# S5 input tables: the two subtractions per table half moved from VectorE into accumulating transposes on TensorE

## The chip, the cores and the metric

The kernel runs on one core of one Trainium2 chip. The metric is the device time of one execution in microseconds (us). TensorE is PE in the profile, its weight loads are PEld; VectorE is DVE, ScalarE is ACT, GpSimd is POOL, and SyncE, whose queue issues all the DMAs here, is SP or SPq.

## The reference, cut to what matters

One layer of a diffusion backbone on 256 latent and 256 context tokens of width 2048: an S5 mixer (128 groups of 16 channels, 64 complex states each, two directions), a gated output product, and a squared-ReLU MLP.

```python
def s5_scan(u, lam_bar, b_bar, s0, reverse):
    bu = jnp.einsum('btgh,gph->btgp', u, b_bar)
    ...
    _, states = lax.associative_scan(_lin_rec_combine, (a, bu), axis=1, reverse=reverse)
...
    lam_bar, b_bar = s5_discretise(a_re[direction], a_im[direction], log_dt[direction], b_re[direction], b_im[direction])
    st_ctx = s5_scan(uc_ctx, lam_bar, b_bar, s0, reverse)
    s_ctx_final = st_ctx[:, 0] if reverse else st_ctx[:, -1]
    st_lat = s5_scan(uc_lat, lam_bar, b_bar, s_ctx_final, reverse)
    y_lat = y_lat + jnp.einsum('btgp,ghp->btgh', st_lat, c_mat).real
...
    z = jax.nn.gelu(y)
    a, g = jnp.split(z @ w_glu, 2, axis=-1)
    return a * jax.nn.sigmoid(g)
...
x_lat = x_lat + gt1 * rmsnorm(y_lat, norm_mix_post)
x_lat = x_lat + gt2 * rmsnorm(sq_relu_mlp(modulate(rmsnorm(x_lat, ...), sh2, sc2), w1, w2), norm_mlp_post)
```

## The kernel before, in words

The S5 mixer is computed in chunks of 8 tokens (L = 8), so a sequence is 32 chunks. For every chunk position the input matrix of a group is a power of the decay times the input weights; a table of these is built once for each group. The 128 groups are 16 blocks of 8, and a block is worked as two halves of 4 groups. Three units of 4, 6 and 6 blocks share one scan each. In the order in which data flows:

- **Powers.** `Qr` and `Qi` hold the real and imaginary powers (128 partitions x 16 blocks x 8 x 8); ScalarE copies them in place, blocks 0 and 1 first.
- **Input tables (`e`).** For a block, GpSimd makes `s1` = Qr + Qi (tile s1e) and the sum and difference `s2` of the input weights `bcb` (tile s2e). For a half, VectorE makes the complex product with three multiplications and two subtractions, five instructions of 128x512: `k1` = s1 * Br, e1 = Qr * s2[0], e0 = Qi * s2[1], then e0 = k1 - e0 and e1 = k1 - e1 (`e_op`, recorded at the helper's line 122; k1 appears as k).
- **Transposes and strips.** TensorE transposes the four 128x128 pieces of e0 and of e1 into a PSUM tile `tr` each (`e_tr`, line 623), which ScalarE copies to `et`. TensorE also multiplies the same pieces by the output weights `cbd` into `st` (`strip`, line 636); this goes through `sk`, a transpose `wps` (line 649) and `W` to DRAM (`wd`), and comes back as the table `it` of a pair of blocks in 8 DMAs (line 689).
- **Scan.** TensorE applies `et` to the tokens (`v`, line 706), ScalarE copies the results into `ctx` and `lat`, and VectorE runs the unit's scan: steps of three dependent instructions (`t`, add, add; lines 727 to 734), five levels over the context and then 31 single steps over the latent chunks.
- **Output.** VectorE makes the output tables `dx` (`dy` for the last two blocks; three multiplications per half, from `bcc`), ScalarE and GpSimd make the sums `sp`, and TensorE adds `it` and `dx` products in `y` (lines 798 and 800). A GELU and a transpose follow.
- **Weights.** Beside all this, weight tiles of 1 MB pass through three `raw` buffers: 64 items for the adaLN products (`ada`, lines 476 and 484) and the items of the gated product (`gb`: line 991 for the first 10 of them, 998 for the rest). The next load of a buffer waits until TensorE has used it. After the gated product comes the MLP.

The order of all instructions up to the MLP is set by a planner (`Plan`): each task has an engine, a duration in us, dependences, a priority, and rings, which stand for buffers that it takes and gives back. The planner runs a list schedule with these numbers and emits the tasks in its order; on the chip each engine then runs its own instructions strictly in that order. The task numbers are estimates in the program and not read from a trace. The ring `e` has 2 buffers, `k1` has 1, `dx` has 4.

Of the kernel before, what the change touches and what calls it, by code (L numbers as in the profile page):

```python
# [8 lines left out]
F32 = mybir.dt.float32  # L9
# [107 lines left out]
def _body(ctx, tc, nc, I, O):  # L117
# [111 lines left out]
    with psx:  # L229
# [55 lines left out]
        sk = ew.tile([128, L, 4, H], F32, name="sk")  # L285
        cbd = [ew.tile([128, 8, 2, 32], F32, name=f"cbd{n}") for n in range(2)]
# [101 lines left out]
        for dst, src in ((Qr, qr), (Qi, qi)):  # L388
            for lower in (True, False):
                q_copy(dst, src, lower, 0, 2)  # L390
        sr = sq.tile([128, C], F32, name="sr")
# [11 lines left out]
        for name, cap in (("ada", 1), ("ev", 1), ("bcb", 2), ("bcs", 2), ("bcc", 2), ("s1e", 2), ("s2e", 1), ("sd", 2), ("cbd", 2),  # L403
                          ("k1", 1), ("dd", 1), ("e", 2), ("et", 2), ("tr", 2), ("st", 1), ("v", 1), ("x", 2), ("yv", 1), ("sk", 1), ("W", 1), ("it", 1),
                          ("ctx", 1), ("lat", 2), ("dx", 4), ("sp", 2), ("z", 1), ("t", 1), ("it2", 1)):
            plan.ring(name, [0.0] * cap)
# [43 lines left out]
        pt = [add("ACT", 0.95, lambda d=d, s=s, g=g, l=l: p_copy(d, s, g, l), prio=PR["p"]) for d, s, g in ((Pr, pr, 1.0), (Pn, pi, -1.0)) for l in (True, False)]  # L450
        t = []
# [138 lines left out]
        def e_sums(b):  # L590
            Bv = bct.pop(("b", b))
            s1 = ew.tile([128, L, 8], F32, tag="s1e", bufs=2, name="s1e")
            tt(SE, s1, Qr[:, b], Qi[:, b], ALU.add)
# [3 lines left out]
            est[b] = Bv, s1, s2  # L597
# [6 lines left out]
        def e_op(b, hf, k):  # L604

            Bv, s1, s2 = est[b]
            hs = slice(hf * 4, hf * 4 + 4)
            n = [128, 4, L, H]
            if k == 0:
                est[b, hf] = (ew.tile([128, 4, L, H], F32, tag="k1e", bufs=1, name="k1"),  # L610
                              ew.tile([128, 2, 4, L, H], F32, tag="e", bufs=2, name="e"))
            k1, e = est[b, hf]
            if k < 3:
                o, p, c = ((k1, s1, Bv[:, 0]), (e[:, 1], Qr[:, b], s2[:, 0]), (e[:, 0], Qi[:, b], s2[:, 1]))[k]
                tt(V, o, p[:, :, hs].rearrange("p t g -> p g t").unsqueeze(3).to_broadcast(n), c[:, hs].unsqueeze(2).to_broadcast(n), ALU.mult)
            else:
                tt(V, e[:, k - 3], k1, e[:, k - 3], ALU.subtract)

        def e_tr(b, hf, r):
            e = est[b, hf][1]  # L620
            est["ps"] = pst("tr", 2)
            for gi in range(4):
                PE.transpose(est["ps"][:, gi * 128:(gi + 1) * 128], e[:, r, gi].rearrange("p s h -> p (s h)"), ident)  # L623
# [7 lines left out]
        def strip(b, hf):  # L631
            e = est[b, hf][1]
# [848 lines left out]
```

## Time and profile before

| | us |
|---|---|
| median of 3 runs (range) | 1312.68 (1308.35 to 1317.29) |
| the profiled execution's own time | 1313.43 |
| its span in the profile | 1311.7 |
| PE busy in the span | 1178.7 (90%) |
| DVE busy | 897.1 (68%) |
| ACT busy | 539.4 (41%) |
| POOL busy | 192.5 (15%) |

Busy shares are averages over very different stages. The input tables are made between 31.7 and 286.5 us of the span; the S5 mixer's last output product ends at 417.3 us, the gated product at 560 us, and the rest is the MLP. The change touches the first of these.

### The profile page before, as it was taken

What the parts mean: (1) busy time and instruction counts of PE and PEld (TensorE: products, weight loads), DVE (VectorE), ACT (ScalarE), POOL (GpSimd) and SP (SyncE); (2) the same over time, 40 slices, a digit from 0 to 9 for tenths busy, and PEclk for the clock granted to TensorE, in tenths of its full rate; (3) what the DMA queues carried; (4) which work ended last, traced back from release to release, by engine and by line L of the source; (5) the groups of instructions that cost most, each with busy time, mean ns of one, the idle gap of its engine ahead of it and who ended that gap; (6) DMA issues with size and microseconds to landing.
All of it is one profiled execution on the core that took longest, in us unless ns stands there. A gap on an engine that the chain in (4) does not pass through costs nothing.

```text
span 1311.7 us, 22524 instructions
## 1 busy us (share of the span) xinstructions
PE 1178.7 (90%) x9457; PEld 957.2 (73%) x9457; DVE 897.1 (68%) x1200; ACT 539.4 (41%) x731; POOL 192.5 (15%) x200
## 2 busy tenths in 40 slices
PE   4576884696898999989999999999999999999997
PEld 1454553452434688989999999999978888888885
DVE  8999999878878677765555565555655555655555
ACT  5442544242115534574333334333434444444443
POOL 4766344611322000030000000000000000000000
PEclk8588997798899999999999999999999999999998
DMA  7488868989986888816656666566656555555552
GB/s 269 148 213 295 316 245 195 307 307 196 260 227 168 319 346 324 317 66 224 234 219 245 217 220 250 209 242 223 230 189 224 192 193 184 182 185 188 192 192 97
DMA packets 74093, 296.68 MB, mean 226 GB/s; under 512 B 7164, under 2 KB 30588, under 8 KB 48520
## 3 DMA queue, kind: packets, MB, share of 16 engines
q1 hardware_dynamic: 73992, 295.25, 66.3%
q8 instruction: 74, 1.21, 0.4%
q14 instruction: 27, 0.22, 0.1%
HBM read 291.15 MB, written 4.07 MB: 225 GB/s over the span
## 4 chain that ended last, share of the span: by engine, by line
PE 74%; DMA 9%; DVE 5%; SPq 1%; ACT 1%; issue 1%; POOL 0%; DVEq 0%; POOLq 0%; ACTq 0%
PE m L1325 27%; PE o L1358 27%; PE gb L998 9%; DMA raw<-wk 4%; PE gb L991 3%; DMA it<-wd 2%; DMA raw<-wa 2%; DVE e L122 2%; SPq L689 1%; PE ada L484 1%; PE y L800 1%; PE v L706 1%; DMA bcc<-bc 1%; PE m L1247 1%; PE ada L476 1%
## 5 line engine op out<-in xcount | busy, mean ns | idle before, releaser
L122 DVE TENSOR_TENSOR wlo<-raw,whi 128x2048 fp32r<-128x2048 f32 x126 | 288.7, 2291 | 134.7 <-ACT whi L125 134.7
L1325 PE MATMUL m<-h,whi 128*128 128x256 f32 x1984 | 248.2, 283 | 0.0
L125 ACT ACTIVATE whi<-raw 128x2048 fp32r<-128x2048 f32 (+1 forms) x130 | 243.8, 1876 | 1.5 <-PE m L1247 1.5
L1325 PEld LDWEIGHTS m<-h,whi 128*128 128x128 f32 x1984 | 242.5, 192 | 0.0
L1358 PE MATMUL o<-wlo,hh 128*128 128x512 f32 x512 | 160.5, 395 | 0.2 <-DVE wlo L122 0.2
L1358 PE MATMUL o<-whi,hh 128*128 128x512 f32 x512 | 160.6, 395 | 0.0
L1358 PE MATMUL o<-whi,hl 128*128 128x512 f32 x512 | 160.5, 395 | 0.0
L1325 PE MATMUL m<-h,wlo 128*128 128x256 f32 x992 | 129.1, 283 | 0.0
L1325 PEld LDWEIGHTS m<-h,wlo 128*128 128x128 f32 x992 | 123.5, 192 | 0.0
L125 ACT ACTIVATE hh<-hid 128x512 fp32r<-128x512 f32 x64 | 40.5, 633 | 194.5 <-PE o L1358 194.5
L125 ACT ACTIVATE r<-m 128x256 f32<-128x256 f32 x64 | 24.6, 384 | 222.9 <-PE m L1325 221.1
L1358 PEld LDWEIGHTS o<-wlo,hh 128*128 128x128 f32 x512 | 95.9, 187 | 24.1 <-DVE wlo L122 0.6
L1358 PEld LDWEIGHTS o<-whi,hh 128*128 128x128 f32 x512 | 95.8, 187 | 24.2 <-ACT hh L125 0.8
L1358 PEld LDWEIGHTS o<-whi,hl 128*128 128x128 f32 x512 | 96.0, 187 | 23.5
L1297 DVE TENSOR_TENSOR hl<-hid,hh 128x512 fp32r<-128x512 f32 x64 | 44.3, 693 | 88.8 <-ACT hh L125 88.7
L1269 DVE TENSOR_TENSOR hid<-r,m 128x256 f32<-128x256 f32 x64 | 26.9, 421 | 91.9 <-ACT r L125 91.9
L991 PE MATMUL gb<-raw,xz 128*128 128x512 f32 x160 | 76.0, 623 | 2.4 <-DMA raw<-wg 2.3
L623 PE MATMUL tr<-ident,e 128*128 128x128 f32 x256 | 44.7, 315 | 30.9 <-DVE e L122 24.6
L998 PE MATMUL gb<-hi,zs 128*128 128x512 f32 (+1 forms) x288 | 70.1, 357 | 0.0
L484 PE MATMUL ada<-raw,cst 128*32 128x512 f32 x256 | 36.9, 654 | 35.4 <-DMA raw<-wk 35.4
L623 PEld LDWEIGHTS tr<-ident,e 128*128 128x128 f32 x256 | 32.5, 160 | 45.8 <-DVE e L122 21.4
L991 PEld LDWEIGHTS gb<-raw,xz 128*128 128x128 f32 x160 | 30.2, 197 | 46.5 <-issue 40.2
(202 smaller groups left out, 1613.2 us busy)
## 6 DMA issues: line engine op xcount, KB each, us to landing
raw<-w SPq DMA_DIRECT2D x128, 1024.0 KB, 4.8
raw<-wk SPq DMA_DIRECT2D x48, 1024.0 KB, 8.4
raw<-wa SPq DMA_DIRECT2D x32, 1024.0 KB, 7.4
raw<-wg SPq DMA_DIRECT2D x32, 1024.0 KB, 5.2
k<-wk SPq DMA_DIRECT2D x16, 1024.0 KB, 7.3
it<-wd SPq DMA_DIRECT2D x64, 128.0 KB, 6.9
xz<-xs SPq DMA_DIRECT2D x4, 1024.0 KB, 9.1
bcb<-bc SPq DMA_DIRECT2D x16, 128.0 KB, 8.9
```

The costliest lines, as they stand in the source:

```text
L122: eng.tensor_tensor(out=out, in0=a, in1=b, op=op)
L125: A.activation(out=out, in_=in_, func=f, **kw)
L476: PE.matmul(adab["a"][32 * j:32 * j + 32, :n], cst[:, 2 * kt:2 * kt + 32], w[:, e, j], start=(kt == 0), stop=(kt == KT - 1))
L484: PE.matmul(adab["k"][32 * j:32 * j + 32, :], cst[:, 2 * kt:2 * kt + 32], w[:, j * 512:(j + 1) * 512], start=(kt == k0), stop=(kt == KT - ...
L623: PE.transpose(est["ps"][:, gi * 128:(gi + 1) * 128], e[:, r, gi].rearrange("p s h -> p (s h)"), ident)
L689: S.dma_start(it[16 * s:16 * s + 16], wdt[b2][:, :, (7 - s) * H:(7 - s) * H + 128])
L991: PE.matmul(banks[p][nk * t + k], xz[kt // BQ][:, GQ * C + (kt % BQ) * T + t * 128:][:, :128], wt[:, (nk * e + k) * 512:(nk * e + k + 1) * ...
L998: PE.matmul(banks[p][nk * t + k][:, :wd], a, w[:, (nk * e + k) * wd:(nk * e + k + 1) * wd], start=ff, stop=ll)
L1269: V.tensor_tensor(out=hid[:, nt], in0=r, in1=ps, op=ALU.mult)
L1297: V.tensor_tensor(out=hl, in0=hid[:, 2 * i:2 * i + 2], in1=hh.bitcast(F32), op=ALU.subtract)
L1325: PE.matmul(ps, w[a][:, kt], (h2h, h2l)[b][:, kt], start=a == b == kt == 0, stop=a == 1 and kt == KT - 1)
L1358: PE.matmul(banks[nh][2 * t + k], w[2 + x][:, e, zz], w[y][:, e * 1024 + k * 512:e * 1024 + k * 512 + 512], start=f and n == 0 and e == es ...
```

## The change

VectorE no longer subtracts. The sums are formed where the pieces are transposed: for each 128x128 piece TensorE transposes k1 and then e on top of it into the same PSUM region, as an accumulating pair. So that a sum serves for the difference, the sum of powers is made with a minus sign, `Qs` = -Qr - Qi, for all blocks in two VectorE instructions (`q_sum`: blocks 0 and 1 at the start, ahead of the reduction `sr`, and blocks 2 to 15 as a task) in place of 16 additions on GpSimd. k1 and both e are then minus what they are to give, and the ScalarE copies out of `v` and `st` scale by -1. The strips take k1 and e as four terms in place of two. The rings change: `k1` has 2 buffers and is given back with `e` after the strips, `s1e` is gone, `dx` has 3 buffers in place of 4. The planner's numbers for the changed tasks change with them (0.43 to 0.9 for a transposing task, 0.57 to 0.8 for a strip), so the order changes throughout the S5 stage.

```diff
--- before.py
+++ after.py
@@ -283,6 +283,7 @@
         V.memset(cst, 0.0)
         V.memset(epst, EPS)
         sk = ew.tile([128, L, 4, H], F32, name="sk")
+        Qs = ew.tile([128, NB, L, 8], F32, name="Qs")
         cbd = [ew.tile([128, 8, 2, 32], F32, name=f"cbd{n}") for n in range(2)]
         for t in cbd:
             GP.memset(t, 0.0)
@@ -388,6 +389,13 @@
         for dst, src in ((Qr, qr), (Qi, qi)):
             for lower in (True, False):
                 q_copy(dst, src, lower, 0, 2)
+
+        def q_sum(b0, b1):
+
+            a, b, o = (w[:, b0:b1].rearrange("p b t g -> p (b t g)") for w in (Qr, Qi, Qs))
+            V.scalar_tensor_tensor(out=o, in0=a, scalar=-1.0, in1=b, op0=ALU.mult, op1=ALU.subtract)
+
+        q_sum(0, 2)
         sr = sq.tile([128, C], F32, name="sr")
         V.tensor_reduce(out=sr, in_=ssum.rearrange("p (a b) -> p b a", b=C), axis=mybir.AxisListType.X, op=ALU.add)
         sr2 = [pst("tr", 2, "sr2") for i in range(2)]
@@ -400,9 +408,9 @@
 
         plan = Plan({"DVE": 25.0, "ACT": 24.4, "Pool": 22.9, "PE": 25.8, "SP": 27.8, "X": 0.0})
         add = plan.add
-        for name, cap in (("ada", 1), ("ev", 1), ("bcb", 2), ("bcs", 2), ("bcc", 2), ("s1e", 2), ("s2e", 1), ("sd", 2), ("cbd", 2),
-                          ("k1", 1), ("dd", 1), ("e", 2), ("et", 2), ("tr", 2), ("st", 1), ("v", 1), ("x", 2), ("yv", 1), ("sk", 1), ("W", 1), ("it", 1),
-                          ("ctx", 1), ("lat", 2), ("dx", 4), ("sp", 2), ("z", 1), ("t", 1), ("it2", 1)):
+        for name, cap in (("ada", 1), ("ev", 1), ("bcb", 2), ("bcs", 2), ("bcc", 2), ("s2e", 1), ("sd", 2), ("cbd", 2),
+                          ("k1", 2), ("dd", 1), ("e", 2), ("et", 2), ("tr", 2), ("st", 1), ("v", 1), ("x", 2), ("yv", 1), ("sk", 1), ("W", 1), ("it", 1),
+                          ("ctx", 1), ("lat", 2), ("dx", 3), ("sp", 2), ("z", 1), ("t", 1), ("it2", 1)):
             plan.ring(name, [0.0] * cap)
         plan.ring("raw", [])
         for n in "bsc":
@@ -448,6 +456,7 @@
         lp_ = wk = drp = None
         qt = [add("ACT", 0.85, lambda d=d, s=s, l=l: q_copy(d, s, l, 2, NB), prio=1) for d, s in ((Qr, qr), (Qi, qi)) for l in (True, False)]
         pt = [add("ACT", 0.95, lambda d=d, s=s, g=g, l=l: p_copy(d, s, g, l), prio=PR["p"]) for d, s, g in ((Pr, pr, 1.0), (Pn, pi, -1.0)) for l in (True, False)]
+        qs = add("DVE", 1.05, lambda: q_sum(2, NB), qt, prio=0)
         t = []
         for m in range(5):
             for k in range(2):
@@ -589,12 +598,10 @@
 
         def e_sums(b):
             Bv = bct.pop(("b", b))
-            s1 = ew.tile([128, L, 8], F32, tag="s1e", bufs=2, name="s1e")
-            tt(SE, s1, Qr[:, b], Qi[:, b], ALU.add)
             s2 = ew.tile([128, 2, 8, H], F32, tag="s2e", bufs=1, name="s2e")
             tt(SE, s2[:, 0], Bv[:, 0], Bv[:, 1], ALU.add)
             tt(SE, s2[:, 1], Bv[:, 0], Bv[:, 1], ALU.subtract)
-            est[b] = Bv, s1, s2
+            est[b] = Bv, s2
 
         def c_diag(b):
             Cv = bct.pop(("s", b))
@@ -603,24 +610,23 @@
 
         def e_op(b, hf, k):
 
-            Bv, s1, s2 = est[b]
+
+            Bv, s2 = est[b]
             hs = slice(hf * 4, hf * 4 + 4)
             n = [128, 4, L, H]
             if k == 0:
-                est[b, hf] = (ew.tile([128, 4, L, H], F32, tag="k1e", bufs=1, name="k1"),
+                est[b, hf] = (ew.tile([128, 4, L, H], F32, tag="k1e", bufs=2, name="k1"),
                               ew.tile([128, 2, 4, L, H], F32, tag="e", bufs=2, name="e"))
             k1, e = est[b, hf]
-            if k < 3:
-                o, p, c = ((k1, s1, Bv[:, 0]), (e[:, 1], Qr[:, b], s2[:, 0]), (e[:, 0], Qi[:, b], s2[:, 1]))[k]
-                tt(V, o, p[:, :, hs].rearrange("p t g -> p g t").unsqueeze(3).to_broadcast(n), c[:, hs].unsqueeze(2).to_broadcast(n), ALU.mult)
-            else:
-                tt(V, e[:, k - 3], k1, e[:, k - 3], ALU.subtract)
+            o, p, c = ((k1, Qs[:, b], Bv[:, 0]), (e[:, 0], Qi[:, b], s2[:, 1]), (e[:, 1], Qr[:, b], s2[:, 0]))[k]
+            tt(V, o, p[:, :, hs].rearrange("p t g -> p g t").unsqueeze(3).to_broadcast(n), c[:, hs].unsqueeze(2).to_broadcast(n), ALU.mult)
 
         def e_tr(b, hf, r):
-            e = est[b, hf][1]
+            k1, e = est[b, hf]
             est["ps"] = pst("tr", 2)
             for gi in range(4):
-                PE.transpose(est["ps"][:, gi * 128:(gi + 1) * 128], e[:, r, gi].rearrange("p s h -> p (s h)"), ident)
+                for n, w in enumerate((k1[:, gi], e[:, r, gi])):
+                    PE.matmul(est["ps"][:, gi * 128:(gi + 1) * 128], w.rearrange("p s h -> p (s h)"), ident, is_transpose=True, start=(n == 0), stop=(n == 1))
             est["ps", b, hf, r] = est["ps"]
 
         def e_ev(b, hf, r):
@@ -629,16 +635,16 @@
             act(ett[b, hf][:, :, r, :], est.pop(("ps", b, hf, r)).rearrange("p (g c) -> p g c", g=4))
 
         def strip(b, hf):
-            e = est[b, hf][1]
+            k1, e = est[b, hf]
             est["st", b, hf] = st = pst("st", 1)
-            for r in range(2):
+            for n, (r, w) in enumerate(((0, k1), (1, k1), (0, e[:, 0]), (1, e[:, 1]))):
                 for j in range(4):
-                    PE.matmul(st[32 * j:32 * j + 32, :128], cbd[b % 2][:, hf * 4 + j, r], e[:, r, j].rearrange("p s h -> p (s h)"),
-                              start=(r == 0), stop=(r == 1))
+                    PE.matmul(st[32 * j:32 * j + 32, :128], cbd[b % 2][:, hf * 4 + j, r], w[:, j].rearrange("p s h -> p (s h)"),
+                              start=(n == 0), stop=(n == 3))
 
         def strip_ev(b, hf):
             lp = 2 * (b % 2) + hf
-            act(sk[:, :, lp], est.pop(("st", b, hf))[:, :128].rearrange("p (s h) -> p s h", h=H))
+            act(sk[:, :, lp], est.pop(("st", b, hf))[:, :128].rearrange("p (s h) -> p s h", h=H), scale=-1.0)
 
         wst, wdt = {}, {}
 
@@ -713,8 +719,8 @@
             cx, lt = views(un)
             pv = vst.pop(("ps", b, hf)).rearrange("p (g r k) -> p k r g", g=4, r=2)
             gu = (b - first_of[un]) * 8 + hf * 4
-            act(cx[:, :, :, gu:gu + 4], pv[:, 0:32])
-            act(lt[:, 1:, :, gu:gu + 4], pv[:, 32:63])
+            act(cx[:, :, :, gu:gu + 4], pv[:, 0:32], scale=-1.0)
+            act(lt[:, 1:, :, gu:gu + 4], pv[:, 32:63], scale=-1.0)
 
         def step_op(un, k, n, m, prev, cur, out):
 
@@ -764,7 +770,7 @@
             if f == 0:
                 ring = d_ring(b)
                 if ring == "dx":
-                    dtab[b, hf] = wk.tile([128, 3, L, 4, H], F32, tag="dx", bufs=4, name="dx")
+                    dtab[b, hf] = wk.tile([128, 3, L, 4, H], F32, tag="dx", bufs=3, name="dx")
                 elif hf == 0:
                     t = lp_.tile([128, 2, 3, L, 4, H], F32, tag=ring, bufs=1 if ring == "ctx" else 2, name="dy")
                     dtab[b, 0], dtab[b, 1] = t[:, 0], t[:, 1]
@@ -813,21 +819,19 @@
             n0 = len(plan.tasks)
             gate = [evt["lat", un - 2]] if PR["gate"] and un > 1 and b == first_of[un] else []
             on_v = PR["sums"] == "DVE"
-            esum = add(PR["sums"], 0.55 if on_v else 1.1, lambda b=b: e_sums(b), ([bcl["b", b]] if b > 1 else []) + gate + (qt if b == 2 else []), prio=1, take=("s1e", "s2e"))
+            esum = add(PR["sums"], 0.55 if on_v else 1.1, lambda b=b: e_sums(b), ([bcl["b", b]] if b > 1 else []) + gate + (qt if b == 2 else []), prio=1, take=("s2e",))
             cb = add("ACT", 0.6, lambda b=b: c_diag(b), [bcl["s", b]] if b > 1 else [], prio=1, take=("cbd",), give=("bcs",))
             for hf in range(2):
                 p = PR["E"]
-                o = [add("DVE", 0.6, lambda b=b, h=hf: e_op(b, h, 0), [esum], prio=p, take=("k1", "e"))]
+                o = [add("DVE", 0.6, lambda b=b, h=hf: e_op(b, h, 0), [esum] + ([qs] if b == 2 else []), prio=p, take=("k1", "e"))]
                 for k in (1, 2):
-                    o.append(add("DVE", 0.6, lambda b=b, h=hf, k=k: e_op(b, h, k), [(o[-1], 0.0)], prio=p))
-                o.append(add("DVE", 0.6, lambda b=b, h=hf: e_op(b, h, 3), [(o[0], 0.13), (o[2], 0.13)], prio=p))
-                o.append(add("DVE", 0.6, lambda b=b, h=hf: e_op(b, h, 4), [(o[3], 0.0), (o[1], 0.13)], prio=p, give=("k1",) + (("s1e", "s2e", "bcb") if hf else ())))
+                    o.append(add("DVE", 0.6, lambda b=b, h=hf, k=k: e_op(b, h, k), [(o[-1], 0.0)], prio=p, give=("s2e", "bcb") if hf and k == 2 else ()))
                 tps, evs = [], []
                 for r in range(2):
-                    tps.append(add("PE", 0.43, lambda b=b, h=hf, r=r: e_tr(b, h, r), [o[3 + r]] + tps, prio=PR["T"], take=("tr",)))
+                    tps.append(add("PE", 0.9, lambda b=b, h=hf, r=r: e_tr(b, h, r), [o[1 + r]] + tps, prio=PR["T"], take=("tr",)))
                     evs.append(add("ACT", 0.48, lambda b=b, h=hf, r=r: e_ev(b, h, r), [tps[r]] + [(x, 0.0) for x in evs], prio=0,
                                    take=("et",) if r == 0 else (), give=("tr",)))
-                sm = add("PE", 0.57, lambda b=b, h=hf: strip(b, h), [o[4], cb] + tps, prio=PR["st"], take=("st",), give=("e",) + (("cbd",) if hf else ()))
+                sm = add("PE", 0.8, lambda b=b, h=hf: strip(b, h), [o[2], cb] + tps, prio=PR["st"], take=("st",), give=("k1", "e") + (("cbd",) if hf else ()))
                 lp = 2 * (b % 2) + hf
                 sv = add("ACT", 0.16, lambda b=b, h=hf: strip_ev(b, h), [sm] + ([(evt["sk"], 0.0)] if lp else []), prio=1, give=("st",), take=("sk",) if lp == 0 else ())
                 evt["sk"] = sv
```

VectorE at the last table half (second half of block 15), before:

```order
L122 TENSOR_TENSOR k_3403<-s1e,bcb 128x512
L734 TENSOR_TENSOR lat<-lat,t 128x96
L122 TENSOR_TENSOR e<-Qr,s2e 128x512
L727 TENSOR_TENSOR t<-ARS,lat 128x192
L122 TENSOR_TENSOR e<-Qi,s2e 128x512
L732 TENSOR_TENSOR lat<-lat,t 128x96
L122 TENSOR_TENSOR e<-k_3403,e 128x512
L734 TENSOR_TENSOR lat<-lat,t 128x96
L122 TENSOR_TENSOR e<-k_3403,e 128x512
L727 TENSOR_TENSOR t<-ARS,lat 128x192
L732 TENSOR_TENSOR lat<-lat,t 128x96
L734 TENSOR_TENSOR lat<-lat,t 128x96
```

The same place with the change:

```order
L738 TENSOR_TENSOR lat<-lat,t 128x96
L740 TENSOR_TENSOR lat<-lat,t 128x96
L733 TENSOR_TENSOR t<-ARS,lat 128x192
L738 TENSOR_TENSOR lat<-lat,t 128x96
L122 TENSOR_TENSOR k_3853<-Qs,bcb 128x512
L740 TENSOR_TENSOR lat<-lat,t 128x96
L122 TENSOR_TENSOR e<-Qi,s2e 128x512
L733 TENSOR_TENSOR t<-ARS,lat 128x192
L122 TENSOR_TENSOR e<-Qr,s2e 128x512
L738 TENSOR_TENSOR lat<-lat,t 128x96
L740 TENSOR_TENSOR lat<-lat,t 128x96
L122 TENSOR_TENSOR dx<-s1d,bcc 128x512
```

The two subtractions (e<-k,e) are gone; four scan instructions stand in a row ahead of the half (lat, lat, t, lat), where before each had a table instruction on either side; and behind the last table two scan adds close the scan of unit 1 and output tables dx follow, where before the scan went on.

TensorE behind the same half, before:

```order
L623 MATMUL tr<-ident,e 128x128 x8
L636 MATMUL st<-e,cbd_146 32x128 x8
L484 MATMUL ada<-raw,cst 32x512 x4
L706 MATMUL v<-xz_78,et 64x64 x16
L649 MATMUL wps<-ident,sk 64x128 x4
```

The same place with the change (the last two of sixteen transposes, and what follows):

```order
L629 MATMUL tr<-ident,k_3853 128x128
L629 MATMUL tr<-ident,e 128x128
L642 MATMUL st<-k_3853,cbd_147 32x128 x8
L642 MATMUL st<-e,cbd_147 32x128 x8
L804 MATMUL y<-it,xz_76 32x8x16 x4
L806 MATMUL y<-dx,sp 32x8x16 x12
```

Each piece is transposed twice (k, then e), a strip has 16 instructions in place of 8, and an output product y of an earlier block now comes right behind the last tables; counted to the last transpose, 59 weight items are used ahead of it and two y blocks more, where it was 53.

VectorE at the start, where the powers are done, before:

```order
L122 TENSOR_TENSOR qi<-qi,c_234 128x16x32
L392 TENSOR_REDUCE sr<-ssum 128x32
L398 RECIPROCAL rs<-rs 128x64
L122 TENSOR_TENSOR k_319<-s1e,bcb 128x512
L122 TENSOR_TENSOR e<-Qr,s2e 128x512
```

The same place with the change:

```order
L122 TENSOR_TENSOR qi<-qi,c_235 128x16x32
L396 SCALAR_TENSOR_TENSOR Qs<-Qr,Qi 128x128
L400 TENSOR_REDUCE sr<-ssum 128x32
L406 RECIPROCAL rs<-rs 128x64
L122 TENSOR_TENSOR k_319<-Qs,bcb 128x512
```

Qs, which reads ScalarE's copies Qr and Qi, stands ahead of the reduction sr, on which the norms of all tokens (rs) wait.

## Rows read from the trace of the kernel before

**Rows 1.** Windows: the table stretch, the output stretch, the next; busy us of each engine.
```profile
core 0: us, PE busy (x) PEld busy (x) DVE busy (x) ACT busy (x) POOL busy (x), PEclk, DMA share, GB/s
31.70:286.50 254.80, 180.04 (x2955) 122.97 (x2949) 239.11 (x478) 105.08 (x241) 135.42 (x124) 0.83 0.78 251
286.50:417.30 130.80, 104.18 (x1057) 52.55 (x1049) 103.74 (x239) 34.18 (x40) 32.00 (x37) 0.93 0.88 216
417.30:436.00 18.70, 18.70 (x41) 6.90 (x41) 14.01 (x19) 11.27 (x17) 0.00 (x0) 1.00 0.74 279
```

**Rows 2.** Chain that ended last, in order of time: start, us, what.
```profile
408.68 6.38 DVE dy L122 x9
...
417.29 8.78 PE gb L991 x20
...
436.02 123.28 PE gb L998 x624
```

**Rows 3.** Waits of PE in 31.7 to 288.5: us, times, longest.
```profile
PE tr L623 <- DVE e L122: 24.6, 15, 7.0
PE ada L484 <- DMA raw<-wk: 21.0, 6, 13.5
```

**Rows 4.** Groups of VectorE instructions, 0 to 420: busy us, mean ns.
```profile
L122 DVE TENSOR_TENSOR e<-k,e 128x512 f32<-128x512 f32 x64 | 48.4, 763 | 0.1
```

**Rows 5.** Timeline of VectorE at the last table half: start us, us, what.
```profile
284.00 0.35 DVE L727 TENSOR_TENSOR t<-ARS,lat 128x192 f32<-128x192 f32 x1
284.27 0.68 DVE L122 TENSOR_TENSOR e<-Qi,s2e 128x512 f32<-128x512 f32 x1
284.87 0.25 DVE L732 TENSOR_TENSOR lat<-lat,t 128x96 f32<-128x96 f32 x1
285.04 0.68 DVE L122 TENSOR_TENSOR e<-k,e 128x512 f32<-128x512 f32 x1
285.64 0.25 DVE L734 TENSOR_TENSOR lat<-lat,t 128x96 f32<-128x96 f32 x1
285.81 0.68 DVE L122 TENSOR_TENSOR e<-k,e 128x512 f32<-128x512 f32 x1
286.41 0.35 DVE L727 TENSOR_TENSOR t<-ARS,lat 128x192 f32<-128x192 f32 x1
286.79 0.26 DVE L732 TENSOR_TENSOR lat<-lat,t 128x96 f32<-128x96 f32 x1
287.08 0.26 DVE L734 TENSOR_TENSOR lat<-lat,t 128x96 f32<-128x96 f32 x1
287.38 0.36 DVE L727 TENSOR_TENSOR t<-ARS,lat 128x192 f32<-128x192 f32 x1
```

**Rows 6.** Timeline of the start: reduction, ScalarE's copies, norms.
```profile
28.68 0.68 DVE L392 TENSOR_REDUCE sr<-ssum 128x32 f32<-128x512 f32 x1
28.80 0.63 ACT L125 ACTIVATE Qi<-qi 64x128 f32<-64x128 f32 x2 [1.30 <-DVE qi L122]
...
31.24 0.55 DVE L398 RECIPROCAL rs<-rs 128x64 f32<-128x64 f32 x1 [1.87 <-ACT rs L125]
```

**Rows 7.** Timeline of PE around a half's transposes and strips (L636).
```profile
286.07 1.06 PE L484 MATMUL ada<-raw,cst 128*32 128x512 f32 x8 [1.10 <-DMA raw<-wk]
287.06 1.09 PE L623 MATMUL tr<-ident,e 128*128 128x128 f32 x8
288.09 0.64 PE L636 MATMUL st<-e,cbd 128*32 128x128 f32 x16
288.55 1.06 PE L484 MATMUL ada<-raw,cst 128*32 128x512 f32 x8
```

**Rows 8.** Timeline of PE: half a block of output products at the higher clock.
```profile
391.26 0.42 PE L798 MATMUL y<-it,xz 128*32 128x128 f32 x8
391.50 0.84 PE L800 MATMUL y<-dx,sp 128*32 128x128 f32 x24
392.16 0.40 PE L798 MATMUL y<-it,xz 128*32 128x128 f32 x8
```

**Rows 9.** Windows of tile tr alone, 31.7 to 288.5.
```profile
31.70:288.50 256.80, 44.73 (x256) 32.52 (x256) 35.95 (x64) 0.83 0.78 250
```

**Rows 10.** Windows of tile st alone, 31.7 to 288.5.
```profile
31.70:288.50 256.80, 22.24 (x512) 13.49 (x512) 0.00 (x0) 8.60 (x31) 0.83 0.78 250
```

**Rows 11.** Waits of VectorE in the output stretch: us, times, longest.
```profile
DVE dx L122 <- PE y L800: 17.3, 4, 6.4
```

## The prediction

> **What bounds the kernel now.** I read the windows first, since the change touches one part of the program, then the chain, then the waits of the two engines that trade work. The profiled execution took 1313.4 us (span 1311.7, so 1.7 us lie around it), 0.7 us above the median of the runs; the sum is made against 1313.4. A measurement of this kernel can hardly tell a change under 1% (13 us) from none.
>
> The reader is to see three stretches in [rows 1]. From 31.7 to 286.5 us the tables are made: VectorE is busy for 239.1 of 254.8 us (94%), TensorE for 180.0 (71%). From 286.5 to 417.3 the last scan and the output products run: VectorE 103.7 of 130.8, TensorE 104.2. Then TensorE is busy without a gap. The chain [rows 2] agrees: the last output tables on VectorE (nine, from 408.68) end just ahead of the gated products at 417.29, and from 436.02 these are one unbroken piece of 123.28 us on TensorE. The change touches nothing after that point, so what it gives or takes is how far 417.3 moves. In the table stretch TensorE's largest wait is for VectorE's tables, 24.6 us in 15 times, and the next for weight loads, 21.0 us in 6 [rows 3]. So VectorE sets the pace there, with TensorE not far behind: removing VectorE work is aimed at the right engine, and the question is what TensorE has left.
>
> **What VectorE loses.** The 64 subtractions [rows 4] last 0.76 us on the mean, but they overlap their neighbours. Start to start such an instruction takes 0.60 us (284.27 to 284.87, 285.81 to 286.41 in [rows 5]), so 64 x 0.60 = 38.4 us go.
>
> **What VectorE gets back.** The large Qs has 896 elements where 0.60 us pass for 512: 1.05 us. The hidden price is cover. In [rows 5] a scan step of three dependent instructions costs 0.27 + 0.17 + 0.17 = 0.61 us where a table instruction stands behind each, and 286.41 to 287.38 = 0.97 us where they stand alone, which is 0.12 us for each pair of scan instructions without an independent one between. In the order of before I count 170 such pairs from the first table to the end of the output tables (40 up to the last table, 130 behind it), in the order with the change 257 (159 and 98): fewer table instructions leave more of the scan uncovered. 87 x 0.12 = 10.4 us. VectorE's work falls by 38.4 - 1.05 - 10.4 = 27 us.
>
> The Trainium skill (VectorE: DVE Perf Modes, Terms) says that a pipeline flush follows every VectorE instruction and the next can't issue until the pipe is empty. By that a scan step would cost the same wherever it stands, the 10.4 us would be nought and the cut 37 us. [Rows 5] do not agree: an instruction that lasts 0.68 us is followed after 0.60 by an independent one, and one of 0.35 only after 0.38 by one that reads its result.
>
> **Where it falls.** The order also moves work over the boundary of the last table. Ahead of it come 49 more scan instructions and 3 fewer output tables, behind it the reverse. Table stretch: -38.4 + 1.05 - 3 x 0.60 + 49 x 0.20 + (159 - 40) x 0.12 = -15 us, to 224 us of VectorE work; with the 15.7 us in which it idles now that is 240 us. Output stretch: -49 x 0.20 - (130 - 98) x 0.12 + 1.8 = -12 us.
>
> **What TensorE gets.** 256 more transposes. At the end of the stretch eight take 287.06 to 288.09 = 1.03 us [rows 7], 0.129 each, so 33 us; the 256 of before keep the engine busy for 44.7 us in all [rows 9], because a part of them ran at the lower clock (the granted clock of the stretch is 0.83 in [rows 1]). The strips double: 288.09 to 288.55 = 0.46 us for a half's 16 records, 15 us for 32 halves, or 22.2 as the ones of before took [rows 10]. Together 48 to 67 us; I take 52, near the lower end, since an engine with fewer gaps should run more of it at the higher clock, as it does in [rows 1] from 417.3 on, where it has no gap and is granted 1.00. Six more weight items come ahead of the last tables (59 for 53), 1.0 us each as the one at 286.07 [rows 7], and two output blocks of two halves at 391.26 to 392.16 = 0.90 us [rows 8]: 9.6 us. So TensorE's work in the table stretch is 180.0 + 52 + 9.6 = 242 us, between 238 and 257. That is as much as VectorE's 240 with its idle time, and TensorE still has to wait for some loads and tables: k1 and e have two buffers each, and both are now held until the strips have run, so either engine can run only two halves ahead. In place of 240 I take 250 us for the stretch, 5 less than now. Most of VectorE's 15 us is thus eaten by TensorE.
>
> The Trainium skill (TensorE: Matmul & The Clock Gate, Part 4: PE-mode transpose) puts a 128x128 transpose at about 275 ns in a kernel and so speaks against the change. [Rows 7] show 0.129 us from one to the next, though one alone takes about that long. By 0.275 the 256 would cost 70 us, TensorE would need 180 + 70 + 15 + 10 = 275 us in the stretch, and the sum would come out at 1313.4 + 20 - 12 + 1 = 1322 us.
>
> **What goes with the rest.** The start: Qs waits for ScalarE's copies, which end at 29.43, and the reduction behind it began at 28.68 before [rows 6]; with Qs itself (under 0.3 us) the norms and the first table come 1.0 us later. GpSimd loses 16 short additions, which cost nothing while VectorE sets the pace. The -1 in the copies rides in the same instruction. Of the output tables' ring, 4 to 3: the second half of a block now needs the block before it finished, where it was the one before that. Waits of VectorE for y are 17.3 us in 4 times now [rows 11]; in the order of SyncE 3 loads of `it` now stand behind the last write of `wd` in place of 5, and 13 weight items are left behind the last tables in place of 19, which shortens what y waits for. I let the two cancel. If the ring wins, the 17.3 could double; if the loads win, 10 may go.
>
> **The sum.** -5 (table stretch) - 12 (output stretch) + 1 (start) = -16: 1313.4 - 16 = 1297 us.
>
> **The rivals.**
> - *TensorE is no obstacle* (VectorE keeps its pace). For it: half of TensorE's idle time is waiting for VectorE or loads, and with denser work more runs at the higher clock. Then -15 - 12 + 1 = -26, 1287 us; with 10 us of the waits for y gone, 1277.
> - *The gain is swallowed*, either by TensorE at its upper 257 us in the table stretch (+2 - 12 + 1 = -9, 1304 us) or by the shorter dx ring (-16 + 17 = +1, 1314 us). For it: VectorE runs in order, so an output table that waits for y holds up the scan behind it, and twelve of them now stand ahead of unit 2's scan. Against it: fewer loads are left at that point.
> - *Slower, TensorE at the lower clock.* If the added pairs run at half the speed of [rows 7], they cost 66 + 30 = 96 us, and TensorE needs 180 + 96 + 9.6 = 286 us in a stretch that takes 255 now: +31 - 12 + 1 = +20, 1333 us. It decides from the point where TensorE's need passes 267 us. For it: the granted clock of 0.83. Against it: the pairs as the ones of before ran [rows 9, 10] give 257, and the engine gets more to do.
>
> **How the numbers follow.** Forecast 1297 (say 1288 to 1304): 0.48, two thirds of it below 1299.6, the bound of 1%. No obstacle: 0.17. Swallowed, 1304 to 1320: 0.24. Slower: 0.11. Faster by over 1%: 0.32 + 0.17 = 0.49; within 1%: 0.16 + 0.24 = 0.40; slower: 0.11. The range leaves out most of the slower case and the best of the first rival: 1279 to 1319.
>
> **What would show each step.** In the changed profile: 64 fewer VectorE instructions at the helper's line, and VectorE busy about 27 us less up to 420 us; lone scan steps at 0.97; the two transposing groups together at 33 to 45 us more; TensorE's busy share of the table stretch above 90% at a clock above 0.83, with its wait for VectorE below the 24.6 us; the last table near 281 us, the first gapless gated product near 401; VectorE's wait for y near 17 us. The prediction is wrong if the last table comes later than before, if the transposed pairs take more than 0.15 us each at the higher clock, or if the waits for y grow by more than 10 us.

## The result and the profile after

The kernel with the change takes 1323.3 us (median of 8 runs, 1319.7 to 1326.9) where the kernel before takes 1311.8 in the same session: ratio 1.0087, 95% interval 1.0063 to 1.0111. It is slower by 11 us; the forecast was 1297 us. The profiled execution took 1322.91 us, its span is 1321.1.

The windows after: the first two stretches of [rows 1] as they were; up to where the last transposes now end (314.5); and the two stretches as they now fall, up to the last table (292.7) and from there to the gated products (427.6):

```profile
core 0: us, PE busy (x) PEld busy (x) DVE busy (x) ACT busy (x) POOL busy (x), PEclk, DMA share, GB/s
31.70:286.50 254.80, 210.21 (x3586) 156.35 (x3581) 207.14 (x446) 103.47 (x232) 107.65 (x106) 0.87 0.78 247
286.50:417.30 130.80, 105.55 (x1096) 56.56 (x1092) 88.63 (x195) 35.14 (x47) 30.46 (x34) 0.93 0.90 214
...
31.70:314.50 282.80, 237.18 (x3986) 173.52 (x3977) 222.95 (x475) 118.75 (x255) 114.33 (x114) 0.88 0.79 250
31.70:292.70 261.00, 216.41 (x3690) 161.18 (x3681) 212.95 (x461) 105.87 (x238) 107.65 (x106) 0.87 0.78 249
292.70:427.60 134.90, 108.32 (x1138) 57.04 (x1137) 92.07 (x192) 36.61 (x45) 36.10 (x40) 0.94 0.86 202
```

Over the same 254.8 us as before VectorE's busy time fell from 239.1 to 207.1 us, TensorE's rose from 180.0 to 210.2. Neither is near full now: 223 and 237 of 282.8 us up to the last transposes, 79% and 84%. The end of the chain of waits, against [rows 2]:

```profile
386.82 13.97 PE gb L995 x32
400.80 0.36 PE y L804 x8
...
419.00 7.29 DVE dy L122 x10
...
427.62 8.78 PE gb L995 x20
...
446.35 13.68 PE gb L1002 x58
```

The last output tables start at 419.00 in place of 408.68, the gated products at 427.62 in place of 417.29, the unbroken ones at 446.35 in place of 436.02. Each step is 10.3 us later, which is the loss but for a microsecond: all of it arises ahead of 419 us. The last table operation on VectorE is here:

```profile
291.10 0.69 DVE L122 TENSOR_TENSOR e<-Qi,s2e 128x512 f32<-128x512 f32 x1
291.97 0.68 DVE L122 TENSOR_TENSOR e<-Qr,s2e 128x512 f32<-128x512 f32 x1
```

It ends at 292.7, 6 us after the old end at 286.5 [rows 1], where 281 was forecast. Who waits, VectorE first (30 to 430 us; us in all, times, longest), then TensorE (31.7 to 314.5):

```profile
DVE dx L122 <- PE y L806: 37.3, 8, 11.8
DVE k L122 <- PE st L642: 30.6, 9, 10.3
```
```profile
PE vp L522 <- DVE r L518: 13.5, 2, 7.2
PE ada L493 <- DMA raw<-wk: 10.8, 5, 4.3
PE ada L485 <- DMA raw<-wa: 6.8, 3, 4.5
```

In [rows 3] TensorE waited 24.6 us for tables; that wait is gone from its list. VectorE waited 2.8 us for strips before:

```profile
DVE e L122 <- PE st L636: 2.8, 2, 2.0
```

Now it waits 30.6 us before it may write k1, until strips have run, and 37.3 us for output products y. The roles are turned round: VectorE has the time that the subtractions took, and spends it waiting for TensorE.

### The profile page after: what moved, and what is told of

Read it like the earlier page. It is cut to its first block, busy times and chain, and to the rows that moved or that the text cites. A ratio compares the mean times of both kernels' runs of the same rounds, so it can differ in the third digit from the quotient of the medians.

```text
span 1321.1 us, 23951 instructions
## 1 busy us (share of the span) xinstructions
PE 1217.9 (92%) x10225; PEld 998.3 (76%) x10225; DVE 860.4 (65%) x1138; ACT 541.8 (41%) x731; POOL 168.7 (13%) x184
## 4 chain that ended last, share of the span: by engine, by line
PE 78%; DMA 9%; DVE 9%; ACT 1%; SPq 1%; issue 1%; POOL 0%; DVEq 0%; POOLq 0%; ACTq 0%
PE m L1329 27%; PE o L1362 27%; PE gb L1002 9%; DMA it<-wd 4%; PE gb L995 3%; DMA raw<-wk 3%; PE tr L629 2%; PE v L712 2%; DMA bcc<-bc 2%; PE ada L493 2%; PE ada L485 1%; PE st L642 1%; DVE e L122 1%; PE y L806 1%; PE m L1251 1%; DVE dx L122 1%
## 5 line engine op out<-in xcount | busy, mean ns | idle before, releaser
L125 ACT ACTIVATE r<-m 128x256 f32<-128x256 f32 x64 | 24.6, 384 | 223.1 <-PE m L1329 221.3
L629 PE MATMUL tr<-ident,k 128*128 128x128 f32 x256 | 64.3, 292 | 0.7 <-ACT et L125 0.7
L629 PE MATMUL tr<-ident,e 128*128 128x128 f32 x256 | 62.1, 284 | 0.0
L1002 PE MATMUL gb<-lo,zs 128*128 128x512 f32 (+1 forms) x208 | 61.1, 359 | 0.0
```

The costliest lines, as they stand in the source:

```text
L125: A.activation(out=out, in_=in_, func=f, **kw)
L629: PE.matmul(est["ps"][:, gi * 128:(gi + 1) * 128], w.rearrange("p s h -> p (s h)"), ident, is_transpose=True, start=(n == 0), stop=(n == 1))
L1002: PE.matmul(banks[p][nk * t + k][:, :wd], a, w[:, (nk * e + k) * wd:(nk * e + k + 1) * wd], start=ff, stop=ll)
```

## The experiments

Ratios are to the kernel before, measured beside each run, with 95% intervals. "Last table" is the end of the last table operation on VectorE in the trace (286.5 before, 292.7 with the change).

**1. The change's order without the added TensorE work.** In the kernel with the change:

```diff
-                for n, w in enumerate((k1[:, gi], e[:, r, gi])):
+                for n, w in enumerate((e[:, r, gi],)):
...
-            for n, (r, w) in enumerate(((0, k1), (1, k1), (0, e[:, 0]), (1, e[:, 1]))):
+            for n, (r, w) in enumerate(((0, e[:, 0]), (1, e[:, 1]))):
```

> The changed kernel in its own order, with the k1 terms left out on TensorE (256 transposes and 256 strip instructions fewer, so the tables are not the reference's). Theory 1, TensorE's added work holds up the tables and through the two buffers of k1 and e also VectorE: the table stretch falls below that of the kernel before, last table near 270 us, time 1290 to 1303. Theory 2, the new order and the shorter dx ring cost the time whatever TensorE does: the output stretch stays as long, time 1314 to 1324.

1318.5 us, 1.0039 (1.0024 to 1.0055); last table 286.9. The time is the second theory's. With VectorE's work cut and none added to TensorE, the kernel is still slower than before, so the doubling can't be all of the loss. It isn't nothing either: without it the kernel is 5 us faster.

**2. The added TensorE work in the old order.** In the kernel before, each transpose is done twice and each strip runs over its two terms twice:

```diff
-                PE.transpose(est["ps"][:, gi * 128:(gi + 1) * 128], e[:, r, gi].rearrange("p s h -> p (s h)"), ident)
+                for n in range(2):
+                    PE.transpose(est["ps"][:, gi * 128:(gi + 1) * 128], e[:, r, gi].rearrange("p s h -> p (s h)"), ident)
...
-            for r in range(2):
+            for r in (0, 1, 0, 1):
```

> The kernel before in its own order, with every transpose and every strip of the input tables run twice (the same result). VectorE keeps its subtractions. Theory 1: TensorE gets the 39 us that the changed kernel's groups show and most of it comes out at the end, 1330 to 1350. Theory 2: TensorE has room, 1312 to 1320.

1323.2 us, 1.0081 (1.0065 to 1.0097); last table 292.6. This lies between the two theories: of some 39 us that the doubling adds to TensorE, 10 come out at the end.

**3. The shorter dx ring alone.** In the kernel before, `dx` has 3 buffers in the planner's ring and in the pool.

```diff
-                          ("ctx", 1), ("lat", 2), ("dx", 4), ("sp", 2), ("z", 1), ("t", 1), ("it2", 1)):
+                          ("ctx", 1), ("lat", 2), ("dx", 3), ("sp", 2), ("z", 1), ("t", 1), ("it2", 1)):
```

> The kernel before with three buffers of dx in place of four, in the ring and in the pool, nothing else (the order follows the ring). Theory 2: VectorE waits longer for y, as the changed kernel shows (45 us for 17), time 1322 to 1335. Theory 1: no difference, 1308 to 1316.

1322.0 us, 1.0066 (1.0048 to 1.0085). One buffer fewer, and nothing else asked for, costs 9 us; the time is the lower end of the first range. VectorE's wait for y grows from 17.3 us [rows 11] to 26.3, and the planner's order changes with the ring: the last table comes at 295.2.

```profile
DVE dx L122 <- PE y L800: 26.3, 6, 9.3
```

Of these, 7.5 us stand ahead of the last table (they end at 238.43 and 253.16), where VectorE waited for no y before.

**4. The change with the old planner numbers** (0.43 and 0.57 for a transposing task and a strip, in place of 0.9 and 0.8).

```diff
-                    tps.append(add("PE", 0.9, lambda b=b, h=hf, r=r: e_tr(b, h, r), [o[1 + r]] + tps, prio=PR["T"], take=("tr",)))
+                    tps.append(add("PE", 0.43, lambda b=b, h=hf, r=r: e_tr(b, h, r), [o[1 + r]] + tps, prio=PR["T"], take=("tr",)))
```

> The changed kernel with the planner's old numbers for the transposing and strip tasks (0.43 and 0.57 for 0.9 and 0.8), so another order with the same work. If it is the new numbers' order that costs (a form of theory 2): 1300 to 1315. If the work itself does (theory 1), or the ring: 1318 to 1330.

1329.8 us, 1.013 (1.0111 to 1.0148), with the last table at 279.5. The time is within the range of the work or the ring. Tables come 13 us earlier than with the change and the end 7 us later: the last table does not set the end by itself, and another number for two tasks moves the time by 7 us.

**5. The subtractions left out of the kernel before**, its order kept.

```diff
-                tt(V, e[:, k - 3], k1, e[:, k - 3], ALU.subtract)
+                pass
```

> The kernel before in its own order with the 64 subtractions left out (the tables lack them), TensorE's work and all rings as they were. The prediction's step, VectorE sets the pace of the table stretch and 0.60 us apiece come back but for the uncovered scan: 1280 to 1290. Rival, the weight stream and TensorE behind it set the pace and VectorE's saving turns into waiting: 1303 to 1314.

1296.7 us, 0.9886 (0.9866 to 0.9906). Free of charge, the removal is worth about 15 us, under half of the 38.4 by which VectorE's work shrinks, and between the two ranges: VectorE sets the pace of the table stretch only in part. The last table comes at 266.3, 20 us earlier, and part of that is lost behind it.

**6. The change with 4 dx buffers.** The room comes from a sum of powers per block (still on VectorE, one operation) in place of `Qs` for all blocks, and from one buffer that `z`, `ev` and `r2` share.

```diff
-                    dtab[b, hf] = wk.tile([128, 3, L, 4, H], F32, tag="dx", bufs=3, name="dx")
+                    dtab[b, hf] = wk.tile([128, 3, L, 4, H], F32, tag="dx", bufs=4, name="dx")
```

> The changed kernel with four buffers of dx again. Room is made by forming the negative sum per block on VectorE into a small tile (16 instructions of 128x64) and by letting the GELU result, ev and r2 share one buffer. If the shorter ring is what costs, as it did alone in the kernel before: 1306 to 1316. If the order behind it and TensorE's work cost: 1318 to 1325.

1316.8 us, 1.0033 (1.0017 to 1.0048): the fourth buffer brings some 7 us of the 11 back. The time lies just above the first range. The last table comes at 291.8, and the waits of VectorE are

```profile
DVE dx L122 <- PE y L801: 34.5, 5, 11.5
DVE k L122 <- PE st L637: 25.9, 10, 9.6
```

**7 and 8. Half the bytes in 64 weight loads**, in the kernel before and in the one with the change (the same edit):

```diff
-            S.dma_start(t if len(shape) == 4 else v, src)
+            if key[0] == "a" or key[:2] in (("k", 2), ("k", 3)):
+                S.dma_start(v[:, :1024], src[:, :1024])
```

> The kernel before with half the bytes in each of the 64 adaLN weight loads ahead of the gated product (the products read the loaded half twice, so the modulation is not the reference's); same instructions on the engines. If the weight stream sets the pace of the S5 stage: 1265 to 1295. If VectorE does: 1303 to 1314.

> The changed kernel with the same half loads. If the weight stream swallowed VectorE's saving, the changed kernel gains more from the half loads than the kernel before does and stands level or ahead: 1255 to 1290, at or under b_half. If TensorE's pairs and the ring cost by themselves, it stays behind b_half by 8 us or more.

1299.7 us, 0.9912 (0.9893 to 0.9931), and 1311.6 us, 0.9989 (0.9973 to 1.0004). The first lies between its two ranges; the second stays 11.9 us behind the first, as expected if the pairs and the ring cost by themselves. Both kernels gain alike, some 12 us each, and the gap between them stays. The bytes of the weights are a cost to both kernels, not the cause of the difference.

**9. The change's work in the old order.** The kernel before, with its plan untouched (the two tasks of the subtractions issue nothing), 4 dx buffers, pairs and four-term strips, `k1` with 2 buffers, room as in 6.

```diff
+                if k == 0 and hf == 0:
+                    est["s1", b] = s1 = ew.tile([128, L, 8], F32, tag="s1e", bufs=1, name="s1e")
+                    V.scalar_tensor_tensor(out=s1, in0=Qr[:, b], scalar=-1.0, in1=Qi[:, b], op0=ALU.mult, op1=ALU.subtract)
...
-            else:
-                tt(V, e[:, k - 3], k1, e[:, k - 3], ALU.subtract)
+            elif k - 3 not in (0, 1):
+                tt(V, e[:, k - 3], k1, e[:, k - 3], ALU.add)
```

> The work of the change (no subtractions, accumulating transposes, four strip terms, negative sum made per block on VectorE) in the order of the kernel before: its planner, task numbers and four buffers of dx are kept, and k1 has two buffers. Order theory: what is left is the measured -16 for the subtractions and at most +10 for TensorE's doubled groups, 1302 to 1310. Work theory (the pairs cost by themselves whatever the order): 1317 to 1325.

1309.1 us, 0.997 (0.9952 to 0.9988): faster than both kernels, by 4 us than the one before, and within the order theory's range. Last table 277.5. Its waits, over the same stretch as above:

```profile
DVE dx L122 <- PE y L804: 21.0, 4, 9.2
DVE k L122 <- PE st L640: 10.6, 6, 4.2
```

Same work, same buffers for k1 and e, and the wait for strips is a third, the wait for y little over half of what they are with the change. Against experiment 6, which has four dx buffers too, they are 10.6 for 25.9 and 21.0 for 34.5 us.

**10. The same with one sum on each engine** (the first by VectorE, the second by pairs, three terms in a strip).

```diff
-                ws = (k1[:, gi], e[:, r, gi]) if r in (0, 1) else (e[:, r, gi],)
+                ws = (k1[:, gi], e[:, r, gi]) if r in (1,) else (e[:, r, gi],)
```

> The same in the same order, with only the second of the two sums made on TensorE; the first stays on VectorE as an addition, and a strip has three terms. If both engines matter in proportion: half of each effect, 1307 to 1312. If TensorE has room for half the pairs: 1300 to 1306.

1312.8 us, 0.9998 (0.9981 to 1.0015). This lies just above both ranges: moving half of the work gives nothing that can be measured; moving all of it gives a little.

**11. The old work in the change's order.** The kernel with the change, both sums by VectorE again, single transposes, two-term strips.

```diff
+            if k:
+                tt(V, o, k1, o, ALU.add)
...
-            for n, (r, w) in enumerate(((0, k1), (1, k1), (0, e[:, 0]), (1, e[:, 1]))):
+            for n, (r, w) in enumerate(((0, e[:, 0]), (1, e[:, 1]))):
```

> The order, the rings (three buffers of dx) and the early sum Qs of the change, but the old work: both sums on VectorE right behind their products, single transposes, two strip terms (the right result). If the new order costs beyond the ring's 9 us: 1328 to 1345. If the ring is all of it: 1318 to 1325.

1348.5 us, 1.0275 (1.0247 to 1.0303). That is above the first range. In this order, moving the sums to TensorE gains 25 us (1348.5 to 1323.3); the order and the ring, with the old work, cost 36 us. The order was planned for the other work, so these two figures are not the parts of the change's loss.

**12. The start of the change's order.** The planner is told that all but the first powers on VectorE are not ready before 36 us, so that `r` comes ahead of them.

```diff
-                t = [add("DVE", 0.55, lambda m=m, k=k: powers(m, k), t, prio=PR["ars"])]
+                t = [add("DVE", 0.55, lambda m=m, k=k: powers(m, k), t, prio=PR["ars"], ready=0.0 if m < 1 else 36.0)]
```

> The kernel with the change, with the planner told that the powers of the scan's decay on VectorE, all but the first pair, are not ready before 36 us of its own time, so that the product r2 of the first adaLN group comes ahead of them; the computation is the same, and the order changes at the start and, less, behind it. Theory A (what the change's order costs beyond the shorter dx ring, some 8 us, comes from the start, where TensorE waits 7.2 us for r behind the powers): r near 43 us in place of 50.1, the last table 5 to 7 us earlier, 1315 to 1319 us, ratio to the kernel before 1.003 to 1.006. Theory B (it comes from the order of the later table stretch, and what the start gives is lost to the next wait of VectorE or TensorE): r earlier as well, but 1321 to 1326 us, ratio 1.007 to 1.011, with the waits for y and for the strips as large as with the change.

1321.7 us, 1.008 (1.0049 to 1.0111). The first r starts at 39.66 in place of 50.09, and the last table ends at 291.9 in place of 292.7. The ten microseconds are gone again by then:

```profile
DVE dx L122 <- PE y L806: 33.7, 8, 11.2
DVE k L122 <- PE st L642: 31.2, 11, 11.1
```

The second theory holds: the waits for strips and for y are what they were, and take up what the start gives.

## Why the prediction was wrong

**The account.** Experiments 9, 6 and the change itself differ by nearly one thing at a time: from before to the new work in the old order 0.997 (-4 us), from there to the change's order, planned with four dx buffers, 1.0033 (+8 us), from there to three dx buffers 1.0087 (+7 us; the place of the sum of powers and of three small tiles differs here too). The sum is the 11 us measured; by the intervals each step is known to some 3 us. Experiments 5 and 2, the two sides of the trade, agree with the first step: -15 and +10 us. So the trade of work that the prediction costed is a small gain, a quarter of the 16 us forecast, and the loss comes from the ring, which it set at nothing, and from the order, of which it counted only the VectorE instructions that change sides of the last table.

**The steps that failed.** The gated products were forecast 16 us earlier and came 10.3 later. In the terms of the sum, 16 of these 26 us are the output stretch (-12 forecast, +4 measured) and 10 the table stretch with the start (-4 forecast, +6 measured); both are taken up below. Beside them stands a term set at nothing: "Of the output tables' ring, 4 to 3 ... I let the two cancel." They did not: the ring alone costs 9 us in the old order (experiment 3) and some 7 in the new one (6). The price in the rival, 17 us, was too high, but the rival named the right place; what it left out is that a ring also sets the order.

**Where the chain shows the new order.** Behind the last table the change's chain of waits runs through SyncE's queue, whose DMAs are issued in order (start, us for all of the group):

```profile
326.36 5.65 SPq L695 DMA_DIRECT2D it<-wd  x8
332.12 0.53 SPq L254 DMA_DIRECT2D bcc<-bc  x1
332.76 0.56 SPq L684 DMA_DIRECT2D wd<-W  x1
333.60 0.34 SPq L189 DMA_DIRECT2D raw<-wk  x1
334.63 12.06 SPq L695 DMA_DIRECT2D it<-wd  x8
347.52 0.33 SPq L254 DMA_DIRECT2D bcc<-bc  x1
348.59 0.54 SPq L189 DMA_DIRECT2D raw<-wg  x1
350.45 12.88 SPq L695 DMA_DIRECT2D it<-wd  x8
```

Three loads of `it` stand close together, and two weight loads pass between 333 and 363 us. Up to 360 us 65 weight loads have been issued, where it was 67 before. This is not the ring's doing alone: with four dx buffers (experiment 6) two of the three loads follow each other without a gap, 16 DMAs in 16.0 us from 333.47 on, and with the shorter ring alone (3) they stand 22 and 21 us apart (331.69, 353.77, 374.36). The items come due on TensorE behind that: in the chain the stretch from the weight load's end to the 13.97 us piece of gated products is 372.85 to 386.82 us, 14.0 us, where before it was 371.37 to 377.36, 6.0 us:

```profile
372.85 1.26 PE ada L493 x8
374.11 6.80 PE gb L995 x12
380.91 1.00 PE ada L493 x8
381.91 1.91 PE gb L995 x4
383.82 1.00 PE ada L493 x8
384.82 1.91 PE gb L995 x4
```
```profile
371.37 1.06 PE ada L484 x8
372.44 1.91 PE gb L991 x4
374.35 1.00 PE ada L484 x8
375.35 1.91 PE gb L991 x4
377.36 13.97 PE gb L991 x32
```

The first fence is the change, the second the kernel before. So 8 of the 10.3 us stand in the chain as weight items that had been done earlier before: ahead of these stretches TensorE has run 60 instructions of gated products, where it was 72. That this delay comes through the order of SyncE's queue is read from the traces; experiments 7 and 8 agree (fewer bytes leave the gap), but none moved the `it` loads alone.

**The other term: "-12 (output stretch)".** It came from counting which instructions the order puts behind the last table. VectorE's busy time there did fall by that much, from 103.7 to 92.1 us, and the stretch grew all the same: from the last table to the gated products it took 417.3 - 286.5 = 130.8 us and now takes 427.6 - 292.7 = 134.9, where 119 was forecast. VectorE waits for y 33.8 us of it, where it was 17.3, and the chain there is mostly DMA loads and TensorE's items. In the eleven traces with whole weight loads whose chain ends this stretch with the same 8.78 us piece of gated products, before and after among them, it takes 129 to 138 us; in none does it come near 119, not even where VectorE's work shrinks and the tables come 20 us earlier (experiment 5: 133).

**The table stretch.** 250 us were forecast, 261 passed (31.7 to 292.7). The work of the two engines was not underrated. VectorE's busy time over the whole span fell from 897.1 to 860.4 us, by 36.7, near the 38.4 - 1.05 of the sum; up to 420 us it is 370.3 to 324.0, but there a part has only moved behind 420. The pairs cost less than the sum took: the tiles `tr` and `st` alone, against [rows 9, 10], are

```profile
31.70:314.50 282.80, 69.70 (x512) 59.87 (x512) 37.90 (x64) 0.88 0.79 250
```
```profile
31.70:314.50 282.80, 36.31 (x1024) 27.67 (x1024) 0.00 (x0) 8.72 (x32) 0.88 0.79 250
```

25.0 and 14.1 us more, 39 in all, where 52 was taken and 33 to 45 named as the sign. The granted clock did not fall (0.88 for 0.83). Wrong was to add a small allowance for waiting to the larger of two busy times. TensorE is busy for 216.4 of the 261.0 us, where 242 was taken, and idles 44.6, where 8 was left; before it idled 74.8 [rows 1]. The two errors cancel in part, and 11 us remain. The engines take turns: with two buffers for k1 and e, VectorE can be two halves ahead, and waits for TensorE where the order has them out of step. The worst one, the 10.3 us at 102.15 (start, us, idle before and who ended it; then TensorE's side):

```profile
102.15 0.69 DVE L122 TENSOR_TENSOR k<-Qs,bcb 128x512 f32<-128x512 f32 x1 [10.29 <-PE st L642]
```
```profile
94.88 1.93 PE L485 MATMUL ada<-raw,cst 128*32 128x256 f32 x16 [4.55 <-DMA raw<-wa]
96.75 1.98 PE L712 MATMUL v<-xz,et 128*64 128x64 f32 x32
98.66 0.48 PE L629 MATMUL tr<-ident,k 128*128 128x128 f32 x1
```

TensorE sat 4.55 us on a weight load, then had an adaLN item and a `v` to do, and only then the transposes and strips that free k1. Before, the subtractions freed k1 on VectorE's own time and VectorE waited 2.8 us for strips in all. The prediction named this hold ("either engine can run only two halves ahead") and priced it, with the loads, at those 8 us. Between experiments 9 and 6, the same work in two orders, the last table moves from 277.5 to 291.8: what the new order costs arises ahead of it.

**By its own signs.** Lone scan steps take 0.97 us, as said (372.28 to 373.26). The start came later, as said (the first table at 32.44 for 31.71, 0.7 us where 1.0 was taken), and a part of it that was not said (r at 50.09 for 42.67, behind powers of about 1.35 us each) proved to cost next to nothing (12). The last table is later than before and the waits for y grew by 20 us (17.3 to 37.3): two of the three signs named for a wrong prediction. TensorE's share of the table stretch, which was to pass 90%, is 83% (216.4 of 261.0). The lower-clock rival, the one that ended slower, has the direction right, its time 10 us too high (1333) and its mechanism wrong: the granted clock rose, and the pairs' sum stayed under the forecast's own. In a row of pairs a transpose takes 0.11 us from start to start, though one alone lasts 0.27:

```profile
261.20 0.27 PE L629 MATMUL tr<-ident,e 128*128 128x128 f32 x1
261.31 0.27 PE L629 MATMUL tr<-ident,k 128*128 128x128 f32 x1
261.42 0.27 PE L629 MATMUL tr<-ident,e 128*128 128x128 f32 x1
```

By the 275 ns of the Trainium skill (TensorE: Matmul & The Clock Gate, Part 4: PE-mode transpose) the sum would have been 1322 us, an estimate from the page's figure and near the result. No run here shows that price for a row of transposes, and the agreement in the total is chance.

**What stays open.** Which part of the change's order, after the start, costs the 8 us between experiments 9 and 6: the waits for strips (10.6 against 25.9 us) and for y (21.0 against 34.5) both grow, and they weren't separated. Behind the last table the stretch is even 6 us shorter in experiment 6 (131.4 for 137.7), so the queue of SyncE above may matter less than the chain suggests. And whether the range of orders that such a planner can give for the same work, with its ends in experiments 4 and 9, has a better one.

## What to carry to other kernels

Where a planner writes the order, a change of work, of a buffer count and of a task's number are three changes: run the new work in the old order first, and the buffer change alone. A buffer given up to make room is a term of the sum with a price (9 us here), even if the place it serves waits little. And where two engines feed each other through two buffers, neither's busy time is the length of the stretch: count who must have finished what before a buffer is free, and what stands ahead of that on the other engine.

## What was not expected of the hardware

- In accumulating pairs a transpose costs no more than a plain one: eight take 1.03 us to the start of what follows (261.03 to 262.06), as eight plain ones do in [rows 7]. Inside a row it is 0.11 us from start to start (261.20 to 261.31), and 0.21 in a row that runs at half of that pace (99.14 to 99.35).
- SyncE's issue of the 8 DMAs of an `it` load takes 5.4 to 8.6 us in six of the change's eight loads and 12.1 and 12.9 us in two; for that time nothing else in the queue starts. In the kernel before seven take 5.1 to 6.1 us and one, with no other `it` load near, 12.4 (295.22). Each of the three long ones began within 2 us of the issue of a weight load (294.74, 333.60, 348.59), but so did one of 7.4 (304.76); the cause was not looked for.
- VectorE's small operations on the powers take 1.17 to 1.37 us each from 38.16 to 48.3 us, while GpSimd runs `xz` products (38.11 to 48.22), and 0.22 to 0.28 from 48.29 on, when that run has ended. That GpSimd's run is the cause was not tested; in the kernel before one such operation takes 0.28 us (47.66) inside a run of GpSimd.
